# A transformer block on one core: convolution sums moved to PSUM, gate projections issued earlier, expert selection in fewer and wider vector operations

## The chip, the cores and the metric

The kernel runs on one core of a Trainium2 chip. The metric is the device time of one execution in microseconds (us), the median of the runs that are shown. Five engines run their own instruction streams and wait for each other: PE (matrix products), DVE and POOL (elementwise work), ACT (elementwise functions and scaling), and SP (starts most transfers).

## What is computed

One encoder layer over 512 tokens of width 1024, all in float32, followed by a retrieval layer over 16384 one-neuron experts:

```python
h = rmsnorm(x)
z = h @ w_in            # [conv input 2*1024 | q 16x64 | k 4x64 | v 4x64 | 2 gates 2*1024]
u = z[:1024] * sigmoid(z[1024:2048])
u = depthwise_conv(u, width=31) + bias;  u = silu(layernorm(u));  A = u @ w_pw
B = windowed_attention(q, k, v, |t-s| <= 128, ALiBi bias, sink) @ w_o
x = x + (sigmoid(gate_A) * A + sigmoid(gate_B) * B) @ w_out
# retrieval: 8 heads, two keys of 128 each
q = rmsnorm(x) @ w_query;  sc = q . sub_keys            # (t, head, 2, 128)
vals, idx = top_k(sc, 16)                                # per key
top_s, pos = top_k(vals0[:, None] + vals1[None, :], 16)  # of 16x16 pairs
expert = idx0[pos // 16] * 128 + idx1[pos % 16];  gate = softmax(top_s)
x = x + sum_k gate_k * gelu(u[expert_k] . h) * v[expert_k]
out = rmsnorm(x)
```

## The kernel before

Every float32 product is made of three passes (`mm3`, lines 61 to 66): both operands are split into a rounded part `hi` (ACT, line 58) and the rest `lo` (line 59, on POOL, on DVE in some places), and PE sums hi·hi, hi·lo and lo·hi in PSUM. One projection of 128 columns (`proj`, line 167) is 24 matmuls of 512 columns.

**Front.** `glu(i)` (line 191) projects the two halves of a 128-channel block of the convolution input, and DVE multiplies them into `ub` (line 200). `conv(pair, ubs)` (line 203) then makes 31 taps for two channel blocks in turn, one DVE instruction per tap and block:

```python
DVE.scalar_tensor_tensor(acc, ub[:, j:j + S], tapt[:, i, j:j + 1], acc,
                         op0=OP.mult, op1=OP.add)          # acc = cv[:, i, :], in SBUF
```

Eight blocks give 240 of these (line 211) and 8 first taps (line 208). Between the pairs stand the projections of k, v (lines 215 to 233) and q (`qproj`, line 235). `attend(g, b)` (line 253) is attention for four heads and 128 queries: scores to PSUM (`s`), a DVE custom instruction that adds the bias and takes the maximum (line 267), exponentials on ACT (275), a scaling by the reciprocal sum on DVE (282), transposes on PE (287) and the product with v (`o`). The bias tables are made on POOL (line 250). Behind attention come the layer norm of the convolution, 16 gate projections (`gate`, line 240, evicted by ACT into `sg`), the projections with `w_o` and `w_pw` (lines 350 and 388) and the output projection (`out_half`).

**Retrieval, preparation.** `qproj2` and `score` fill `sct` per head. For tokens 128 to 511, DVE finds the top 16 (`topk`), and `select(t, q)` (line 469) turns positions into expert indices by a one-hot table `oh` of 16 positions by 64 entries, once per key: compare (487), multiply by the index (490), sum (496). `build(t)` (line 570) makes one-hot rows for 8 tokens (594, 595), scales them (596, 597), and PE multiplies them into gate tables, which go to DRAM.

**Retrieval, main part.** All 128 blocks of experts are multiplied for these tokens (`u_block`, `v_block`): 30 u blocks run ahead, beside the preparation. For tokens 0 to 127 rows are gathered instead (`step`).

Order of work: a scheduler orders each engine's stream by priority in program order, and an engine then runs its stream in order. `tc.high_priority()` moves a few DVE operations ahead. [...]

## Time and profile before

| | us |
|---|---|
| three runs | 1873.26, 1873.43, 1878.59 |
| median | 1873.43 |
| profiled execution, its own time | 1870.83 |
| its span (first to last instruction) | 1869.1 |

| stretch of the span | what PE does |
|---|---|
| to 27.75 | load, first norm, first glu |
| 27.75 to 275 | projections; DVE convolves |
| 275 to 406.6 | attention; DVE's last convolution taps are at 286; gate projections in between |
| 406.6 to 520.9 | rest of the gates, w_o, w_pw |
| 520.9 to 595 | output projection, second norm |
| 595 to 912 | query projections, top-k, selection, one-hot tables |
| 912 to the end | expert blocks and gathered rows |

A row of the profile gives an instruction group's line, engine, operation, the tile written and the tiles read, its shape and count, its busy time, the mean time of one, and the idle time just ahead of it with what ended it.

### The profile page before, as it was taken

The numbers are of one execution on the slowest core, as the hardware profiler recorded it, in microseconds if no ns is written. First come the engines' busy times: TensorE is split into PE (matmuls) and PEld (weight loads), VectorE is DVE, ScalarE is ACT, GpSimd is POOL, SyncE is SP. The second block draws the span as 40 slices with busy tenths as digits, with TensorE's granted clock in tenths as the row PEclk, the third lists the DMA queues.
The fourth block names the chain that finished last, engine by engine and source line by source line (L and its number), as shares of the span: only waits on it lengthen the run. The fifth ranks groups of instructions, "written<-read, shape, count | busy, mean of one in ns | idle before, by whom it ended". The sixth has DMA issues, their size and how long they took to land.

```text
span 1869.1 us, 25289 instructions
## 1 busy us (share of the span) xinstructions
PE 1751.3 (94%) x8873; PEld 1495.0 (80%) x8873; DVE 1536.5 (82%) x2649; ACT 753.2 (40%) x1329; POOL 1049.0 (56%) x757
## 2 busy tenths in 40 slices
PE   7878879999999986887899999999999999999998
PEld 5656656778887876776889899999999999999886
DVE  5999978854534999999798899998988977797874
ACT  4222325865224414554443333333333333333243
POOL 4544373231015525465535788788887888787611
PEclk9999889999999999999999999999999999999999
DMA  4122111034234202468866989898998888887972
GB/s 152 58 77 75 61 46 35 12 92 167 68 102 150 88 26 93 137 191 253 275 221 239 340 320 337 297 330 317 325 336 306 330 311 316 313 314 292 351 270 97
DMA packets 148943, 379.43 MB, mean 203 GB/s; under 512 B 11520, under 2 KB 63760, under 8 KB 148816
## 3 DMA queue, kind: packets, MB, share of 16 engines
q1 hardware_dynamic: 110832, 241.20, 37.2%
q0 software_dynamic: 37120, 134.52, 20.3%
q10 hardware_dynamic: 864, 2.10, 0.3%
q8 instruction: 69, 1.13, 0.2%
q14 instruction: 58, 0.48, 0.1%
HBM read 346.84 MB, written 30.93 MB: 202 GB/s over the span
## 4 chain that ended last, share of the span: by engine, by line
PE 40%; DVE 14%; DMA 5%; issue 2%; POOL 2%; ACT 1%; SPq 0%; POOLq 0%; DVEq 0%; ACTq 0%
PE acc L65 7%; PE acc L66 7%; PE acc L64 7%; PE hps L66 6%; PE hps L64 6%; PE hps L65 6%; DVE oi L594 1%; DVE ohi L596 1%; DVE olo L597 1%; DVE oj L595 1%; DVE vlo L59 1%; DMA row<-in_v_dram,eidx 1%; DMA vraw<-in_v_dram 1%; DVE ij L496 1%; POOL ulo L59 1%
## 5 line engine op out<-in xcount | busy, mean ns | idle before, releaser
L59 POOL TENSOR_TENSOR ulo<-uraw,uhi 128x512 fp32r<-128x512 f32 x256 | 423.8, 1671 | 279.7 <-ACT uhi L58 262.9
L64 PE MATMUL hps<-big,uhi 128*128 128x384 f32 x1024 | 350.9, 343 | 7.8 <-ACT hb L429 7.7
L66 PE MATMUL hps<-big,ulo 128*128 128x384 f32 x1024 | 350.2, 342 | 2.6 <-POOL ulo L59 2.6
L65 PE MATMUL hps<-big,uhi 128*128 128x384 f32 x1024 | 349.4, 341 | 0.0
L59 POOL TENSOR_TENSOR wlo<-wraw,whi 128x512 fp32r<-128x512 f32 x120 | 194.8, 1631 | 231.5 <-ACT whi L58 205.6
L65 PE MATMUL acc<-vlo,ph 128*128 128x512 f32 x768 | 300.2, 391 | 2.0 <-DVE vlo L59 2.0
L64 PE MATMUL acc<-vhi,ph 128*128 128x512 f32 x768 | 298.9, 390 | 1.2 <-ACT vhi L58 1.2
L66 PE MATMUL acc<-vhi,pl 128*128 128x512 f32 x768 | 299.6, 390 | 0.0
L64 PE MATMUL mm<-big,whi 128*128 128x512 f32 x544 | 224.2, 412 | 28.0 <-DVE ub L200 12.4
L58 ACT ACTIVATE uhi<-uraw 128x512 fp32r<-128x512 f32 x256 | 155.5, 629 | 206.7 <-DMA uraw<-in_ut_dram 83.9
L641 DVE SCALAR_TENSOR_TENSOR yacc<-row,dots,yacc 128x1024 f32<-128x1024 f32 x127 | 189.2, 1490 | 58.0 <-DMA row<-in_v_dram,eidx 57.7
L66 PE MATMUL mm<-big,wlo 128*128 128x512 f32 x544 | 220.2, 405 | 14.5 <-POOL wlo L59 14.4
L630 DVE SCALAR_TENSOR_TENSOR row<-row,h2tok 128x1024 f32<-128x1024 f32 x128 | 193.9, 1521 | 34.6 <-DMA row<-in_u_dram,eidx 33.9
L58 ACT ACTIVATE vhi<-vraw 128x1024 fp32r<-128x1024 f32 x128 | 135.0, 1055 | 212.3 <-DMA vraw<-in_v_dram 200.2
L65 PE MATMUL mm<-big,whi 128*128 128x512 f32 x544 | 220.0, 404 | 0.0
L211 DVE SCALAR_TENSOR_TENSOR cv<-ub,tapt,cv 128x512 f32<-128x512 f32 x240 | 212.1, 930 | 1.8
L58 ACT ACTIVATE whi<-wraw 128x512 fp32r<-128x512 f32 x152 | 94.7, 631 | 287.4 <-PE mm L65 169.7
L64 PEld LDWEIGHTS hps<-big,uhi 128*128 128x128 f32 x1024 | 195.1, 191 | 15.4 <-ACT hb L429 8.7
L623 POOL DMA_INDIRECT row<-in_v_dram,eidx x128 | 176.3, 1377 | 49.3 <-DVE yacc L641 20.3
L623 POOL DMA_INDIRECT row<-in_u_dram,eidx x128 | 182.9, 1429 | 33.1 <-issue 17.5
L65 PEld LDWEIGHTS hps<-big,uhi 128*128 128x128 f32 x1024 | 195.5, 191 | 4.1
L66 PEld LDWEIGHTS hps<-big,ulo 128*128 128x128 f32 x1024 | 194.8, 190 | 3.6 <-POOL ulo L59 3.6
(217 smaller groups left out, 3027.0 us busy)
## 6 DMA issues: line engine op xcount, KB each, us to landing
uraw<-in_ut_dram SPq DMA_DIRECT2D x128, 512.0 KB, 7.1
vraw<-in_v_dram SPq DMA_DIRECT2D x128, 512.0 KB, 5.5
gates_dram<-st SPq DMA_DIRECT2D x12, 2048.0 KB, 9.9
gt<-gates_dram SPq DMA_DIRECT2D x32, 768.0 KB, 7.0
wraw<-in_w_in_dram SPq DMA_DIRECT2D x44, 512.0 KB, 3.3
wraw<-in_w_query_dram SPq DMA_DIRECT2D x16, 512.0 KB, 3.4
oraw<-in_w_out_dram SPq DMA_DIRECT2D x16, 256.0 KB, 3.1
wraw<-in_w_o_dram SPq DMA_DIRECT2D x8, 512.0 KB, 3.8
```

Source lines behind the costliest of these rows:

```text
L58: ACT.activation(hi, src, AF.Copy)
L59: lo_engine.tensor_tensor(lo, src, f(hi), op=OP.subtract)
L64: PE.matmul(ps, wh, mh, start=first and i == 0, stop=False)
L65: PE.matmul(ps, wh, ml, start=False, stop=False)
L66: PE.matmul(ps, wl, mh, start=False, stop=last and i == n - 1)
L211: DVE.scalar_tensor_tensor(acc, ub[:, j:j + S], tapt[:, i, j:j + 1], acc, op0=OP.mult, op1=OP.add)
L496: DVE.tensor_reduce(ij[t][:, s, hs, :].rearrange("p h k -> p (h k)"), oh.rearrange("p a h k -> p (h k) a"), AX.X, OP.add)
L594: DVE.tensor_tensor(prs(oi), iota8, row(0), op=OP.is_equal)
L595: DVE.tensor_tensor(prs(oj), iota8, row(1), op=OP.is_equal)
L623: POOL.indirect_dma_start(out=row, out_offset=None, in_=table, in_offset=bass.IndirectOffsetOnAxis(ap=eidx[:, c:c + 1], axis=0))
L630: DVE.scalar_tensor_tensor(row, row, 1.0, h2tok, op0=OP.mult, op1=OP.mult, accum_out=dots[:, c:c + 1])
L641: DVE.scalar_tensor_tensor(yacc, row, dots[:, c:c + 1], yacc, op0=OP.mult, op1=OP.add)
```

## The change

1. The convolution's running sum lives in PSUM (pool `psc`, two banks); only the last tap writes `cv` in SBUF. `glu` takes its two PSUM tiles from attention's score pool. The pool `pso` for attention's output is opened only after all convolutions, in `psc`'s place.
2. `glu` of the next pair stands ahead of `conv` of this one; the 16 gate projections are spread: 11 between the convolutions (`fill`), 5 within attention.
3. The bias tables go from POOL to ACT, and half of the scalings by the reciprocal sum from DVE to ACT.
4. `select` handles both keys in one compare, one multiply and one sum, with the 16 positions innermost (neighbouring) in `oh`; the index to compare with is written twice in a row (`fd`).
5. `build` joins the two compares into one of 2048 elements.

```diff
         def proj(src, rhs, ws=None, lo_engine=POOL, ps=None):
...
-            pso = ac.enter_context(tc.tile_pool(name="pso", bufs=1, space=PSUM))
-
             glup = ExitStack()
+            psc = glup.enter_context(tc.tile_pool(name="psc", bufs=2, space=PSUM))
...
-                pa = proj(w_in[i], hT, first if i == 0 else None)
-                pg = proj(w_in[8 + i], hT)
+                pa = proj(w_in[i], hT, first if i == 0 else None, ps=psa.tile([P, S], F32, name="s"))
+                pg = proj(w_in[8 + i], hT, ps=psa.tile([P, S], F32, name="s"))
...
             def conv(pair, ubs):
+                accs = [psc.tile([P, S], F32, name="ca") for _ in pair]
                 for j in range(TAPS):
-                    for i, ub in zip(pair, ubs):
-                        acc = cv[:, i, :]
+                    for i, ub, acc in zip(pair, ubs, accs):
...
-                            DVE.scalar_tensor_tensor(acc, ub[:, j:j + S], tapt[:, i, j:j + 1], acc,
-                                                     op0=OP.mult, op1=OP.add)
-
-            conv((0, 1), [glu(0), glu(1)])
+                            DVE.scalar_tensor_tensor(cv[:, i, :] if j == TAPS - 1 else acc, ub[:, j:j + S],
+                                                     tapt[:, i, j:j + 1], acc, op0=OP.mult, op1=OP.add)
+
+            ub01 = [glu(0), glu(1)]
+            conv((0, 1), ub01)
+            ub23 = [glu(2), glu(3)]
...
-                    POOL.tensor_scalar(bt[:, i, :], dist, -8.0 * slope, None, op0=OP.mult)
+                    ACT.activation(bt[:, i, :], dist, AF.Copy, scale=-8.0 * slope)
...
                 for i in range(4):
-                    DVE.tensor_scalar(L[:, i, :n], L[:, i, :n], rd[:, i:i + 1], None, op0=OP.mult)
+                    if i % 2:
+                        ACT.activation(L[:, i, :n], L[:, i, :n], AF.Copy, scale=rd[:, i:i + 1])
+                    else:
+                        DVE.tensor_scalar(L[:, i, :n], L[:, i, :n], rd[:, i:i + 1], None, op0=OP.mult)
...
-            conv((2, 3), [glu(2), glu(3)])
+            gates = [gate_of for k in range(KD) for gate_of in (KD + k, k)]
+
+            def fill(n):
+                for _ in range(n):
+                    gate(gates.pop(0))
+
             for i in range(4):
                 qproj(i)
-            conv((4, 5), [glu(4), glu(5)])
+            conv((2, 3), ub23)
+            ub45 = [glu(4), glu(5)]
             for i in range(4, 8):
                 qproj(i)
-            conv((6, 7), [glu(6), glu(7)])
+            fill(3)
+            conv((4, 5), ub45)
+            ub67 = [glu(6), glu(7)]
+            fill(6)
+            conv((6, 7), ub67)
+            fill(2)
+            glup.close()
+            pso = ac.enter_context(tc.tile_pool(name="pso", bufs=1, space=PSUM))
             for g in range(4):
                 make_bias(g)
                 for b in range(NT):
                     attend(g, b)
-            glup.close()
+                    if b == 1 or (g, b) == (0, 3):
+                        fill(1)
...
-            for k in range(KD):
-                gate(KD + k)
             sigmoid(1)
-            for k in range(KD):
-                gate(k)
...
-            DVE.tensor_tensor(fa, fa, bits[:, 0:2, :], op=OP.add)
...
-            for s in range(2):
-                oh = sel.tile([P, TOPK, HH, TOPK], F16, name="oh", bufs=2)
-                DVE.tensor_tensor(oh.rearrange("p a h k -> p a (h k)"), iota16,
-                                  fa[:, s, None, :].to_broadcast([P, TOPK, nk]), op=OP.is_equal)
...
-                DVE.tensor_reduce(ij[t][:, s, hs, :].rearrange("p h k -> p (h k)"),
-                                  oh.rearrange("p a h k -> p (h k) a"), AX.X, OP.add)
+            fd = sel.tile([P, 2, nk, 2], F16, name="fd", bufs=2)
+            DVE.tensor_tensor(fd, fa[:, :, :, None].to_broadcast([P, 2, nk, 2]),
+                              bits[:, 0:2, :, None].to_broadcast([P, 2, nk, 2]), op=OP.add)
...
+            oh = sel.tile([P, 2, HH, TOPK, TOPK], F16, name="oh", bufs=2)
+            DVE.tensor_tensor(oh.rearrange("p s h k (a b) -> p (s h k) a b", b=2),
+                              iota16.rearrange("p (a b) -> p a b", b=2)[:, None].to_broadcast([P, 2 * nk, TOPK // 2, 2]),
+                              fd.rearrange("p s n b -> p (s n) b")[:, :, None, :].to_broadcast([P, 2 * nk, TOPK // 2, 2]),
+                              op=OP.is_equal)
+            oh3 = oh.rearrange("p s h k a -> p (s h) k a")
+            DVE.tensor_tensor(oh3, oh3, ixf.rearrange("p s h a -> p (s h) a")[:, :, None, :]
+                              .to_broadcast([P, 2 * HH, TOPK, TOPK]), op=OP.mult)
+            DVE.tensor_reduce(ij[t][:, 0:2, hs, :].rearrange("p s h k -> p s (h k)"),
+                              oh.rearrange("p s h k a -> p s (h k) a"), AX.X, OP.add)
...
-                    DVE.tensor_tensor(prs(oi), iota8, row(0), op=OP.is_equal)
-                    DVE.tensor_tensor(prs(oj), iota8, row(1), op=OP.is_equal)
-                    DVE.tensor_tensor(prs(oh_), prs(oj), row(2), op=OP.mult)
-                    DVE.tensor_tensor(prs(ol), prs(oj), row(3), op=OP.mult)
+                    DVE.tensor_tensor(prs(oij), iota8, rows(0), op=OP.is_equal)
+                    for s in range(2):
+                        DVE.tensor_tensor(prs(ohl)[:, s * TB8:(s + 1) * TB8], prs(oij)[:, TB8:],
+                                          rows(2)[:, s * TB8:(s + 1) * TB8], op=OP.mult)
```

What moves, in the order in which the engines issue. DVE of the kernel before, where the scores of the first attention block meet the convolution of blocks 4 and 5 (`L,m<-s` is the bias and maximum, `ub<-mm` the product of a glu):

```order
L211 SCALAR_TENSOR_TENSOR cv<-ub,tapt,cv 128x512 x13
L267 ISA L,m<-s,bias,sinkt 128x256
L267 ISA m 128x1
L200 TENSOR_TENSOR ub<-mm,sgm 128x512
L211 SCALAR_TENSOR_TENSOR cv<-ub,tapt,cv 128x512
L208 TENSOR_SCALAR cv<-ub,tapt,dwb 128x512
L211 SCALAR_TENSOR_TENSOR cv<-ub,tapt,cv 128x512 x6
```

These attention operations stood between the taps; in the change none does. DVE of the change, the last pair of blocks and the first attention operation:

```order
L209 SCALAR_TENSOR_TENSOR ca<-ub,tapt,ca 128x512 x13
L198 TENSOR_TENSOR ub<-s,sgm 128x512
L209 SCALAR_TENSOR_TENSOR ca<-ub,tapt,ca 128x512
L206 TENSOR_SCALAR ca<-ub,tapt,dwb 128x512
L209 SCALAR_TENSOR_TENSOR ca<-ub,tapt,ca 128x512 x30
L209 SCALAR_TENSOR_TENSOR cv<-ub,tapt,ca 128x512
L209 SCALAR_TENSOR_TENSOR ca<-ub,tapt,ca 128x512 x14
L209 SCALAR_TENSOR_TENSOR cv<-ub,tapt,ca 128x512
L267 ISA L,m<-s,bias,sinkt 128x256
```

Before, 120 of the 248 taps stood ahead of the first attention operation and 128 among attention; now all 248 stand ahead of it. PE's stream follows: before, 432 projection matmuls precede the first score, now 936; within attention it holds 144 (511 before), and after attention 360 of the front's (497 before).

ACT of the change, from the last q projection (`qh`) to the sigmoids of the last two glus (`sgm`); `sg` are gate evictions, `whi` weight splits:

```order
L57 ACTIVATE qh<-mm 128x512
L57 ACTIVATE whi<-wraw 128x512 x2
L242 ACTIVATE sg_83<-mm 128x512
L57 ACTIVATE whi<-wraw 128x512 x2
L242 ACTIVATE sg_82<-mm 128x512
L57 ACTIVATE whi<-wraw 128x512 x2
L242 ACTIVATE sg_83<-mm 128x512
L57 ACTIVATE whi<-wraw 128x512 x4
L193 ACTIVATE sgm<-s 128x512
L57 ACTIVATE whi<-wraw 128x512 x4
L193 ACTIVATE sgm<-s 128x512
```

Three gate evictions stand ahead of the last two glus, and eight more follow them before the first exponential; before the change no gate came ahead of the last glu.

## Rows read from the trace of the kernel before

**Rows 1.** The page: busy time of PE and DVE, and three rows of 40 slices.

```profile
PE 1751.3 (94%) x8873; PEld 1495.0 (80%) x8873; DVE 1536.5 (82%) x2649; ACT 753.2 (40%) x1329; POOL 1049.0 (56%) x757
...
PE   7878879999999986887899999999999999999998
...
DVE  5999978854534999999798899998988977797874
...
PEclk9999889999999999999999999999999999999999
```

**Rows 2.** Windows: start:end, length, then busy us (instructions) of each engine; PEclk.

```profile
core 0: us, PE busy (x) PEld busy (x) DVE busy (x) ACT busy (x) POOL busy (x), PEclk, DMA share, GB/s
27.75:275.00 247.25, 202.94 (x807) 156.65 (x806) 230.51 (x291) 61.17 (x105) 124.35 (x74) 0.91 0.20 67
275.00:406.60 131.60, 130.23 (x602) 90.76 (x602) 113.00 (x309) 94.40 (x227) 34.56 (x25) 1.00 0.09 28
406.60:520.90 114.30, 114.30 (x500) 93.51 (x500) 46.49 (x70) 49.74 (x76) 18.05 (x14) 1.00 0.37 121
520.90:595.00 74.10, 72.26 (x343) 59.38 (x342) 28.36 (x44) 30.79 (x60) 24.35 (x19) 1.00 0.42 142
...
640.00:912.00 272.00, 224.59 (x1634) 193.69 (x1633) 266.72 (x680) 120.35 (x220) 141.34 (x94) 0.94 0.47 142
...
950.00:1850.00 900.00, 897.98 (x4467) 808.26 (x4467) 770.22 (x878) 338.92 (x537) 649.82 (x452) 1.00 0.84 304
```

**Rows 3.** PE's waits from 25 to 275 us: total us, times, longest.

```profile
PE mm L66 <- POOL wlo L59: 13.9, 1, 13.9
PE mm L64 <- DVE ub L200: 12.4, 4, 6.7
PE mm L64 <- DVE ql L59: 8.0, 5, 3.1
```

**Rows 4.** DVE's longest wait in the same stretch.

```profile
DVE ql L59 <- ACT qh L58: 13.4, 1, 13.4
```

**Rows 5.** Line 211, the taps: ns minimum/median/maximum.

```profile
L211 DVE SCALAR_TENSOR_TENSOR cv<-ub,tapt,cv x240: 733/747/1789, 30.5 to 286.3; 128x512 f32<-128x512 f32 x120
```

**Rows 6.** DVE's timeline: start us, us in all, instructions; three runs of taps.

```profile
30.53 14.68 DVE L211 SCALAR_TENSOR_TENSOR cv<-ub,tapt,cv 128x512 f32<-128x512 f32 x14
...
56.27 4.71 DVE L211 SCALAR_TENSOR_TENSOR cv<-ub,tapt,cv 128x512 f32<-128x512 f32 x7
...
231.34 23.94 DVE L211 SCALAR_TENSOR_TENSOR cv<-ub,tapt,cv 128x512 f32<-128x512 f32 x36
```

**Rows 7.** POOL's timeline: weight splits, a lone one and four around 235 us.

```profile
53.16 1.38 POOL L59 TENSOR_TENSOR wlo<-wraw,whi 128x512 fp32r<-128x512 f32 x1 [0.95 <-ACT whi L58]
...
234.52 26.50 POOL L59 TENSOR_TENSOR wlo<-wraw,whi 128x512 fp32r<-128x512 f32 x4 [7.74 <-ACT whi L58]
```

**Rows 8.** Groups by line and shape: DVE operations that read PSUM.

```profile
L200 DVE TENSOR_TENSOR ub<-mm,sgm 128x512 f32<-128x512 f32 x8 | 5.5, 684 | 8.3 <-ACT sgm L195 8.3
L104 DVE SCALAR_TENSOR_TENSOR big<-mm,g,big 128x512 fp32r<-128x512 f32 x8 | 5.4, 747 | 2.7 <-ACT big L103 2.7
```

**Rows 9.** Groups: the reciprocal scaling, and a comparable operation on ACT.

```profile
L282 DVE TENSOR_SCALAR L<-L,rd 128x384 f32<-128x384 f32 x32 | 16.1, 553 | 0.1
L275 ACT ACTIVATE L<-L,nm 128x384 f32<-128x384 f32 x32 | 19.3, 610 | 1.3 <-DVE nm L270 1.1
```

**Rows 10.** Selection's operations: ns minimum/median/maximum.

```profile
L487 DVE TENSOR_TENSOR oh<-iota,fa x16: 671/690/1787, 647.0 to 990.2; 128x1024 f16<-128x1024 f16 x16
L490 DVE TENSOR_TENSOR oh<-oh,ixf x16: 1211/1220/2315, 648.2 to 993.0; 128x1024 f16<-128x1024 f16 x16
L496 DVE TENSOR_REDUCE ij<-oh x16: 1847/2022/2074, 650.5 to 996.1; 128x64 f32<-128x1024 f16 x16
L503 DVE TENSOR_REDUCE gs<-ij x8: 204/210/223, 654.4 to 987.3; 128x4 f32<-128x64 f32 x8
```

**Rows 11.** The one-hot compare of the table build, in the same form.

```profile
L594 DVE TENSOR_TENSOR oi<-iotar,tt x48: 677/683/1792, 748.0 to 907.1; 128x1024 f16<-128x1024 f16 x48
```

More of the change, by code (lines that the diff above doesn't have):

```diff
@@ L37 @@
 UQ, UB = 2, 4
-SELE = "DD"
 LAST = 3
@@ L165, in encoder_block, with proj @@
         hT = [(hT_hi[:, k, :], hT_lo[:, k, :]) for k in range(KD)]
-        def proj(src, rhs, ws=None, lo_engine=POOL):
+        def proj(src, rhs, ws=None, lo_engine=POOL, ps=None):
             ws = ws or weights(src, lo_engine)
-            ps = psm.tile([P, S], F32, name="mm")
+            ps = psm.tile([P, S], F32, name="mm") if ps is None else ps
             mm3(ps, ws, rhs)
@@ L481, in select @@
             DVE.tensor_tensor(fa, fa, bits[:, 4, None, :].to_broadcast([P, 2, nk]), op=OP.mult)
-            DVE.tensor_tensor(fa, fa, bits[:, 0:2, :], op=OP.add)
-            ixf = sel.tile([P, HH, 2, TOPK], F16, name="ixf", bufs=2)
-            DVE.tensor_copy(ixf, idxs[t][:, hs])
-            for s in range(2):
-                oh = sel.tile([P, TOPK, HH, TOPK], F16, name="oh", bufs=2)
-                DVE.tensor_tensor(oh.rearrange("p a h k -> p a (h k)"), iota16,
-                                  fa[:, s, None, :].to_broadcast([P, TOPK, nk]), op=OP.is_equal)
-                if SELE[q] == "D":
-                    DVE.tensor_tensor(oh, oh, ixf[:, :, s, :].rearrange("p h a -> p a h")[:, :, :, None]
-                                      .to_broadcast([P, TOPK, HH, TOPK]), op=OP.mult)
-                else:
-                    for h in range(HH):
-                        POOL.tensor_tensor(oh[:, :, h, :], oh[:, :, h, :],
-                                           ixf[:, h, s, :, None].to_broadcast([P, TOPK, TOPK]), op=OP.mult)
-                DVE.tensor_reduce(ij[t][:, s, hs, :].rearrange("p h k -> p (h k)"),
-                                  oh.rearrange("p a h k -> p (h k) a"), AX.X, OP.add)
@@ L573, in build, with twice @@
                 PE.transpose(tp[:, s, :], ij[t][:, s].rearrange("p h k -> p (h k)"), ident)
-            def twice(ap):
-                return ap[..., None].to_broadcast(list(ap.shape) + [2])
-            tt = gw.tile([P, 4, P, 2], F16, name="tt", bufs=2)
-            ACT.activation(tt[:, 0:2], twice(tp[:, 0:2, :]), AF.Copy)
-            ACT.activation(tt[:, 2], twice(tp[:, 2, :]), AF.Copy, scale=GSC)
-            DVE.scalar_tensor_tensor(tt[:, 3], twice(tp[:, 2, :]), GSC, tt[:, 2], op0=OP.mult, op1=OP.subtract)
+            def twice(s):
+                a = tp[:, s, :].rearrange("p (g t) -> p g t", t=TB8)
+                return a[..., None].to_broadcast([P, P // TB8, TB8, 2])
+            tt = gw.tile([P, P // TB8, 4, TB8, 2], F16, name="tt", bufs=2)
+            for s in range(3):
+                ACT.activation(tt[:, :, s], twice(s), AF.Copy, scale=1.0 if s < 2 else GSC)
+            DVE.scalar_tensor_tensor(tt[:, :, 3], twice(2), GSC, tt[:, :, 2], op0=OP.mult, op1=OP.subtract)
             for c in range(P // GT):
@@ L585, in build, with rows @@
                     n = c * GT + q8 * TB8
-                    oi, oj, oh_, ol = (gw.tile([P, TB8, NKEY], F16, name=nm, bufs=2) for nm in ("oi", "oj", "ohi", "olo"))
-                    def row(s):
-                        return tt[:, s, n:n + TB8, None, :].to_broadcast([P, TB8, NKEY // 2, 2])
+                    oij, ohl = (gw.tile([P, 2, TB8, NKEY], F16, name=nm, bufs=2) for nm in ("oij", "ohl"))
+                    def rows(s):
+                        a = tt[:, n // TB8, s:s + 2].rearrange("p s t b -> p (s t) b")
+                        return a[:, :, None, :].to_broadcast([P, 2 * TB8, NKEY // 2, 2])
                     def prs(a):
-                        return a.rearrange("p t (a b) -> p t a b", b=2)
-                    DVE.tensor_tensor(prs(oi), iota8, row(0), op=OP.is_equal)
-                    DVE.tensor_tensor(prs(oj), iota8, row(1), op=OP.is_equal)
-                    DVE.tensor_tensor(prs(oh_), prs(oj), row(2), op=OP.mult)
-                    DVE.tensor_tensor(prs(ol), prs(oj), row(3), op=OP.mult)
+                        return a.rearrange("p s t (a b) -> p (s t) a b", b=2)
+                    DVE.tensor_tensor(prs(oij), iota8, rows(0), op=OP.is_equal)
+                    for s in range(2):
+                        DVE.tensor_tensor(prs(ohl)[:, s * TB8:(s + 1) * TB8], prs(oij)[:, TB8:],
+                                          rows(2)[:, s * TB8:(s + 1) * TB8], op=OP.mult)
                     for q4 in range(TB8 // 4):
```

13 lines of the change are left out of this document (7 added, 6 removed).

## The prediction

> **What bounds the kernel now.** I read the page first: PE is busy 94% of the span and DVE 82%, and the slices show that they take turns [rows 1]. From 25 to about 275 us and again from 640 to 910 us DVE stands at 9 while PE falls to 6 to 8; elsewhere PE stands at 9. Then I cut the span into stretches [rows 2]. [...] From 275 to 595 us PE is busy practically without a gap. From 640 to 912 us DVE works 267 of 272 us and PE 225. From 950 us on PE is busy 898 of 900 us; so whatever is saved ahead of that shifts the rest forward by as much, and nothing in the change touches the rest.
>
> **Why DVE is slow in the first stretch.** Of the 240 taps the fastest take 733 ns, the slowest 1789 [rows 5]. Seven of them take 4.71 us, 0.67 each from start to start, in a stretch where POOL is idle (its weight split ends at 54.5 us, the next starts after 62); fourteen beside POOL's weight splits take 14.68 us, 1.05 each [rows 6, 7]. At 231 us DVE runs 36 taps without a gap at 0.665 each, and in that time POOL needs 26.5 us for four splits, against 1.4 us for one [rows 6, 7]. PE waits 13.9 us for the last of them, and DVE itself then 13.4 us for attention behind it [rows 3, 4]. So an operation with two SBUF inputs on DVE and POOL's splits hold each other up, in both directions. DVE's operations with one input in PSUM show no such spread: the glu product takes 684 ns [rows 8].
>
> **The change part by part.** The sum is made against the profiled execution, 1870.8 us; the median of the runs shown is 2.6 us above it.
>
> *Taps in PSUM.* 240 taps keep their number; 232 now read and write PSUM and the last of each block writes SBUF. No row has DVE writing PSUM. Nearest is line 104, the same operation with a PSUM input and an SBUF output, 747 ns [rows 8], 14 ns above the fastest tap [rows 5]. From below, a tap can cost 0.60 from start to start (the shortest step in these rows: 684 ns of the glu product less the 0.08 by which successive operations overlap: 747 against 0.67); from above 1.05, as beside POOL today. I take 0.70, near line 104. [...]
>
> *Projections up to attention.* In the change's order, 936 projection matmuls stand before the first score, 48 of them done at 27.75 us as now. The other 888, with the 8 transposes of v, at the pace of a full PE (500 in 114.3 us, 0.2286 each [rows 2]) take 204.8 us. A glu needs its tiles back from DVE before the next one starts; before, PE lost 12.4 us to that in four waits [rows 3], and I charge 10 us. So PE would reach the first score at 27.75 + 204.8 + 10 = 242.6 us. DVE has until then: it starts at 30 us and has 240 taps of 0.70 plus about 20 us of first taps, glu products and lo parts (some 30 operations of about 0.65), which ends at 218 us without waits. The last glu is ready at about 199 us (242.6 less eight gates of 24 x 0.2286); 47 taps follow it, to 232 us. So PE is the bound here, as long as a tap costs under 0.80 (by DVE's whole work) to 0.93 us (by the last 47 taps). Eleven gates hide DVE's taps instead of standing alone later.
>
> *Attention.* In the change it holds 144 projection matmuls, 192 scores, 160 transposes, 120 products with v and 20 records of the layer norm's matmuls (the trace shows each as two): 636. The present stretch of that kind made 602 in 131.6 us, 0.2186 each [rows 2]; so 139 us. DVE gets lighter: no taps among its operations, and 32 of the 64 scalings, 553 ns for the wider ones, leave [rows 9]. ACT gets 32 scalings and 16 bias tables, at about 0.6 us each going by its exponential [rows 9], some 29 us on top of 94 of 132 us [rows 2], less about 11 us of layer norm work that now comes after attention: 112 of 139. I add 7 us for the waits that this closeness brings, as no row prices them. The bias tables leave POOL, which was no bound there (35 of 132 us).
>
> *After attention.* 360 matmuls of w_o and w_pw at 0.2286 take 82.3 us, and 12 records of the layer norm 2.7. The rest of the layer norm (about 20 us on DVE and ACT) runs beside the 168 matmuls of w_o (38 us), as does the first sigmoid. The output projection starts at 242.6 + 139 + 7 + 85 = 473.6 instead of 520.9 us: **47 us earlier**. From there to 595 us nothing changes.
>
> *Selection.* Six of the eight calls lie in the DVE-bound stretch up to 912 us; the other two lie beside a full PE and cost nothing either way. Compare and multiply work on the same 1024 elements; the first makes two a step (neighbours in 16 bits), the second one: 671 and 1211 ns [rows 10]. The difference, 540 ns for 512 steps, is 1.05 ns a step, and 131 ns are fixed. In the change both have neighbouring positions, so both take 1024 steps for 2048 elements: 1211 ns. The sum over positions reads them 128 bytes apart today, 1847 ns at best: 1.68 ns a step [rows 10]. The small contiguous sum of line 503 gives (210 - 131) / 64 = 1.2 ns a step. For 2048 that is between 2.59 and 3.56 us; I take 2.6, since the new layout is contiguous like line 503's. Doubling the indices (`fd`, 256 elements instead of 128, one a step) adds about 0.14. A call goes from 2 x (0.67 + 1.21 + 1.85) = 7.46 to 1.21 + 1.21 + 2.6 + 0.14 = 5.16: 2.3 us saved, 14 us for six. At the upper price of the sum it is 1.3 a call, 8 us. Each operation may also lose 1.1 us to POOL (the maxima of the compare [rows 10]), and there are three instead of six of them: up to 7 us more. [...]
>
> *Table build.* 48 times two compares of 683 ns [rows 11] become one of 1211: 0.155 us by durations, about 0.07 from start to start since neighbours overlap by 0.08. Between 3 and 7 us; I take 3. The two remaining multiplications stay, and so do POOL's splits, which hold up whatever runs beside them. PE has 47 us free in the DVE-bound stretch [rows 2], so 17 us come through.
>
> Sum: 1870.8 - 47 - 14 - 3 = 1807 us in the profiled execution, 1809 for the median.
>
> **The rivals.**
> 1. *Attention becomes the bound.* Today its chains (scores, maximum, exponential, scaling, transposes, split) are filled by 511 projection matmuls and partly hidden under the taps; the change leaves 144 and none of the taps. For it: ACT at 112 of 139 us. Against: DVE has less to do, and PE's stretch held without idle time. If an instruction costs 0.26 instead of 0.2186, 26 us are lost: 1835 us for the median.
> 2. *The taps still collide with POOL.* Only if it is not the second SBUF input that collides. Then the mean of today, 930 ns or so between 0.67 and 1.05, stays: taps end at 50 + 223 = 273 us, the output projection starts 231 us later, at 504: 17 + 17 us gained, 1839 us for the median. Against it: the steady 684 ns of [rows 8].
> 3. *Slower: a running sum in PSUM is dear.* Each tap reads what another wrote two instructions ago, now through PSUM, and attention can no longer start before the last tap, as it does today. The output projection starts at 281 + 240 p; with the 17 us of the second part, the change loses when p exceeds 1.07 us. At 1.5 us it starts at 641: 1870.8 + 120 - 17 = 1974 us, 1976 for the median. For it: no row has DVE writing PSUM. Against it: line 104 reads PSUM for 14 ns.
> 4. *PE keeps its full pace throughout.* Without the 17 us of waits I charged and with attention's matmuls at 0.2 each (12 us), the upper ends of selection (7) and build (4) on top: 40 us below the forecast, 1769 us.
>
> **How the numbers follow.** The forecast gets 0.60; rival 1 0.15, rival 2 0.09, rival 4 0.09, rival 3 0.05, and 0.02 that a wait cancels everything. The forecast's own unknowns are -10 (the lower end of selection and waits) to +15 us (rival 4's terms in part). The range of 8 in 10 reaches from rival 4's end to rivals 1 and 2 with a few us of spread, 1770 to 1842 us, and leaves out rival 3. Faster by over 0.3% (5.6 us, about what a measurement of this kernel tells from no change): 0.60 + 0.15 + 0.09 + 0.09, about 0.92; slower 0.05; the same 0.03.
>
> **What would show it.** Right: taps with minimum and maximum within 50 ns of each other, at about 0.75 us; POOL's splits at 1.3 us with no 26 us group; the first score at about 243 us on PE and the output projection near 474; selection's sum as one operation of 2.3 to 2.7 us, its multiplication at 1.2; the stretch of tables about 17 us shorter; from there the same 920 us or so to the end. Wrong: taps over 1 us (rivals 2 and 3, told apart by their spread); PE idle in attention behind ACT or DVE (rival 1); a sum of 3.5 us. The prediction is off in its mechanism if the front ends before 520 us for another reason than PE's closed gaps, or if the time saved ahead of 950 us is not found at the end.

## The result, and the profile after

The changed kernel takes 1815.0 us (median of four runs, 1813.0 to 1818.5) against 1876.0 us for the kernel before on the same chip (four runs: the three shown above and 1880.7): a ratio of 0.967, 95% interval 0.965 to 0.970. The forecast was 1809 us, with a range of 1770 to 1842. On another chip (e11 below) the changed kernel took 1813.0 us, and the kernel before stood between 1872.2 and 1873.2 us in all three groups of experiments; so their medians are compared with 1813.0.

The page of the changed kernel, for [rows 1]: busy time, and three rows of 40 slices.

```profile
PE 1734.4 (96%) x8873; PEld 1484.2 (82%) x8873; DVE 1432.8 (79%) x2545; ACT 770.8 (43%) x1374; POOL 961.4 (53%) x741
...
PE   6999999989999978888999999999999999999998
...
DVE  4999856674536999999989987887787777878874
...
PEclk8999999999999989999999999999999999999999
```

In the first third PE now stands at 9 nearly throughout, and DVE only in the second to the fourth slice. The seven and the four eights of PE under the nines of DVE (634 to 860 us) are still there. The windows of the same kernel, cut where its own stages end, answer to [rows 2]:

```profile
0.00:27.75 27.75, 13.54 (x52) 10.76 (x53) 9.50 (x20) 15.86 (x29) 11.28 (x26) 0.82 0.54 180
...
27.75:243.50 215.75, 210.56 (x926) 172.12 (x925) 183.60 (x271) 65.34 (x113) 99.12 (x85) 1.00 0.28 93
243.50:382.90 139.40, 136.99 (x637) 95.64 (x637) 92.72 (x289) 113.37 (x274) 9.05 (x7) 1.00 0.07 23
382.90:477.40 94.50, 90.81 (x374) 70.71 (x373) 53.54 (x78) 41.19 (x65) 10.51 (x8) 0.98 0.36 117
...
477.40:551.50 74.10, 72.93 (x347) 60.18 (x347) 28.39 (x45) 31.50 (x61) 24.30 (x19) 1.00 0.42 142
...
597.00:855.00 258.00, 217.83 (x1619) 186.65 (x1618) 257.88 (x675) 119.32 (x220) 120.56 (x98) 0.96 0.49 151
...
892.00:1792.00 900.00, 898.39 (x4470) 808.54 (x4469) 728.77 (x822) 341.13 (x536) 640.30 (x449) 1.00 0.83 303
```

Up to the first score PE works 210.6 of 215.8 us at the full clock (before: 202.9 of 247.3 at 0.91), in attention 137.0 of 139.4. The 74.1 us behind the start of the output projection and the 900 us to the end hold the same work as before (347 and 4470 records of PE against 343 and 4467 [rows 2]; a record is one matmul in the trace). PE's one wait in the second window is this:

```profile
PE s L63 <- ACT sgm L193: 5.2, 5, 1.0
```

The 13.9, 12.4 and 8.0 us of [rows 3] are gone; what is left is a wait for the sigmoid of a glu on ACT. The groups of line or shape, ns minimum/median/maximum, first and last start, of taps (209), scores and output projection (63), selection (501 to 508) and table build (607, 609):

```profile
L209 DVE SCALAR_TENSOR_TENSOR ca<-ub,tapt,ca x232: 735/752/756, 37.0 to 233.7; 128x512 f32<-128x512 f32 x116
L209 DVE SCALAR_TENSOR_TENSOR cv<-ub,tapt,ca x8: 739/745/748, 73.4 to 234.5; 128x512 f32<-128x512 f32 x8
...
L63 PE MATMUL s<-kh,qh x64: 275/381/442, 243.5 to 364.3; 64*128 64x256 f32 x32, 64*128 64x384 f32 x32
...
L63 PE MATMUL mm<-ohi,qh x64: 389/392/486, 477.4 to 521.7; 128*128 128x512 f32 x64
...
L501 DVE TENSOR_TENSOR oh<-iota,fd x8: 1201/1214/2331, 602.8 to 914.1; 128x2048 f16<-128x2048 f16 x8
...
L506 DVE TENSOR_TENSOR oh<-oh,ixf x8: 1201/1212/2187, 604.1 to 918.4; 128x2048 f16<-128x2048 f16 x8
...
L508 DVE TENSOR_REDUCE ij<-oh x8: 2260/2270/2272, 605.5 to 920.6; 128x128 f32<-128x2048 f16 x8
...
L607 DVE TENSOR_TENSOR oij<-iotar,tt x48: 1209/1214/2320, 687.6 to 847.6; 128x2048 f16<-128x2048 f16 x48
...
L609 DVE TENSOR_TENSOR ohl<-oij,tt x96: 665/680/1769, 691.8 to 850.4; 128x1024 f16<-128x1024 f16 x96
```

The taps' spread of 733 to 1789 ns [rows 5] has become 735 to 756. The output projection starts at 477.4 instead of 520.9 us, 43.4 us earlier; the profiled execution is 57.9 us shorter (1870.8 to 1813.0), so 14.5 us come from behind it.

### The profile page after: what moved, and what is told of

Same layout as the page of the kernel before. It is cut to its first block, busy times and chain, and to the rows that moved or that the text cites. A ratio compares the mean times of both kernels' runs of the same rounds, so it can differ in the third digit from the quotient of the medians.

```text
span 1811.2 us, 25192 instructions
## 1 busy us (share of the span) xinstructions
PE 1734.4 (96%) x8873; PEld 1484.2 (82%) x8873; DVE 1432.8 (79%) x2545; ACT 770.8 (43%) x1374; POOL 961.4 (53%) x741
## 4 chain that ended last, share of the span: by engine, by line
PE 68%; DVE 15%; issue 2%; DMA 2%; ACT 1%; POOL 1%; SPq 0%; POOLq 0%; DVEq 0%; ACTq 0%
PE acc L64 8%; PE acc L63 8%; PE acc L65 8%; PE hps L65 7%; PE hps L64 7%; PE hps L63 7%; PE mm L63 5%; PE mm L65 5%; PE mm L64 4%; DVE ohl L609 4%; DVE oij L607 3%; DMA row<-in_v_dram,eidx 1%; PE s L63 1%; PE pt L290 1%; PE s L64 1%
## 5 line engine op out<-in xcount | busy, mean ns | idle before, releaser
L58 POOL TENSOR_TENSOR ulo<-uraw,uhi 128x512 fp32r<-128x512 f32 x256 | 406.1, 1595 | 290.6 <-ACT uhi L57 271.0
L58 POOL TENSOR_TENSOR wlo<-wraw,whi 128x512 fp32r<-128x512 f32 x120 | 157.8, 1318 | 203.5 <-ACT whi L57 202.0
L57 ACT ACTIVATE uhi<-uraw 128x512 fp32r<-128x512 f32 x256 | 160.1, 631 | 233.6 <-PE hps L64 140.9
L654 DVE SCALAR_TENSOR_TENSOR yacc<-row,dots,yacc 128x1024 f32<-128x1024 f32 x127 | 177.2, 1396 | 69.7 <-DMA row<-in_v_dram,eidx 69.4
L58 DVE TENSOR_TENSOR vlo<-vraw,vhi 128x1024 fp32r<-128x1024 f32 x128 | 188.6, 1474 | 18.9 <-ACT vhi L57 18.9
L636 POOL DMA_INDIRECT row<-in_v_dram,eidx x128 | 165.1, 1290 | 48.7 <-DVE yacc L654 21.5
L57 ACT ACTIVATE ph<-hb 128x384 fp32r<-128x384 f32 x128 | 66.8, 523 | 287.4 <-PE acc L64 274.6
L65 PEld LDWEIGHTS acc<-vhi,pl 128*128 128x128 f32 x768 | 144.2, 188 | 30.9 <-DVE pl L58 0.3
L64 PEld LDWEIGHTS acc<-vlo,ph 128*128 128x128 f32 x768 | 144.2, 188 | 30.0 <-DVE vlo L58 3.7
L63 PEld LDWEIGHTS acc<-vhi,ph 128*128 128x128 f32 x768 | 144.1, 188 | 28.4 <-ACT vhi L57 1.0
```

Of the source, the lines that this page charges most:

```text
L57: ACT.activation(hi, src, AF.Copy)
L58: lo_engine.tensor_tensor(lo, src, f(hi), op=OP.subtract)
L63: PE.matmul(ps, wh, mh, start=first and i == 0, stop=False)
L64: PE.matmul(ps, wh, ml, start=False, stop=False)
L65: PE.matmul(ps, wl, mh, start=False, stop=last and i == n - 1)
L636: POOL.indirect_dma_start(out=row, out_offset=None, in_=table, in_offset=bass.IndirectOffsetOnAxis(ap=eidx[:, c:c + 1], axis=0))
```

## The experiments

The theory on trial: the sum in PSUM frees DVE and POOL from each other; PE then bounds the front, as long as the gates are there to fill it; selection and build save about what their durations say. A starting time of the output projection (start, below) is the start of line 63's group with `ohi`, in the profiled execution; of the same kernel it was 477.4 and 480.4 us, so 3 us of it mean nothing. For the tables there is a second measure: from start to the first product of `v_block` (first start of `acc<-vhi,ph`) it takes 412.5 us in the kernel before, 397.8 and 397.2 in the two traces of the changed kernel, and 397.7 to 399.8 in the seven runs below that leave the tables alone (e1, e2, e5, e6, e8, e9, e10). From there to the last product every run takes 921 to 930 us.

**e1, the taps' sum back in SBUF.**

```diff
-  scalar_tensor_tensor(cv[:, i, :] if j == TAPS - 1 else acc, ub[:, j:j + S], tapt[:, i, j:j + 1], acc, ...)
+  scalar_tensor_tensor(acc if j == TAPS - 2 else cv[:, i, :], ub[:, j:j + S], tapt[:, i, j:j + 1],
+                       acc if j == TAPS - 1 else cv[:, i, :], ...)
```

> The changed kernel with the taps' running sum back in SBUF; only the last two taps go through the PSUM tile, so that its bank is held as long as before, and everything else (order, gates, attention, selection, tables) stays. Theory of the prediction: a second SBUF input on DVE and POOL's splits hold each other up, so taps spread from 733 to about 1790 ns with a mean near 0.9 us start to start, POOL's weight splits rise again over 1.5 us, DVE becomes the bound before attention (240 x 0.9 + 20 us from 37 us), the first score falls from 243 to about 270 us, and the time goes from 1815 to about 1842 us (1830 to 1850). Rival, the gain of the front comes from the new order of the projections alone: first score within 4 us of 243, time 1812 to 1819 us.

Measured: 1869.0 us, 56 more than the changed kernel (ratio to before 0.997, 0.996 to 0.999). Its taps, where the front ends, and the window of attention's first 27 us:

```profile
L209 DVE SCALAR_TENSOR_TENSOR cv<-ub,tapt,cv x224: 734/744/1881, 38.3 to 291.5; 128x512 f32<-128x512 f32 x112
...
L209 DVE SCALAR_TENSOR_TENSOR ca<-ub,tapt,cv x8: 747/749/1836, 78.7 to 292.3; 128x512 f32<-128x512 f32 x8
L209 DVE SCALAR_TENSOR_TENSOR cv<-ub,tapt,ca x8: 734/738/748, 80.0 to 293.1; 128x512 f32<-128x512 f32 x8
...
L63 PE MATMUL mm<-ohi,qh x64: 389/392/486, 533.7 to 578.0; 128*128 128x512 f32 x64
```

```profile
283.00:310.00 27.00, 17.29 (x57) 12.86 (x57) 17.09 (x39) 8.25 (x23) 1.81 (x1) 0.62 0.07 20
```

The spread is back with the second SBUF input. The eight taps that read PSUM do not have it (748 at most, in the same stretch, though eight are few); the eight that read SBUF twice and write PSUM do (1836). The theory holds in kind and was too cheap: the first score came at 283 us, not 270, and start is 533.7, 13 us later than before the change. Up to there the new order without the PSUM sum is worse than the old one.

**e2, the gates written behind attention.**

```diff
-            fill(3)            # and fill(6), fill(2), fill(1) in attention
+            for k in range(KD):          # behind the layer norm
+                gate(KD + k)
             sigmoid(1)
+            for k in range(KD):
+                gate(k)
```

> The changed kernel with the sixteen gate projections back behind attention, where the kernel before had them; taps stay in PSUM. Theory of the prediction: the PSUM sum only shortens DVE's work, and the gates have to be there for PE to fill it; without them DVE (240 x 0.67 + 20 us, from 37 us) bounds the front, first score at about 220 to 225 us, attention with 517 records bound by ACT's 110 us of work at about 125 us, then 88 us of gates with the layer norm hidden under them and 85 us up to the output projection: it starts at about 520 instead of 477 us, time 1855 us (1845 to 1875), so nearly all of the 43 us lost. Rival, the PSUM sum is the gain by itself and the gates' place is worth little: 1815 to 1830 us.

Measured: 1811.0 us (0.966, 0.963 to 0.969), no difference to the changed kernel; start 474.5. The theory's number failed, and the time is below the rival's 1815 to 1830 us as well. The evictions of the gates, and two windows about the end of DVE's taps, say why:

```profile
L242 ACT ACTIVATE sg<-mm x16: 578/580/600, 191.0 to 387.2; 128x512 f32<-128x512 f32 x16
```

```profile
200.00:225.00 25.00, 25.00 (x112) 20.71 (x111) 25.00 (x39) 8.12 (x14) 12.19 (x10) 1.00 0.29 94
225.00:250.00 25.00, 25.00 (x104) 16.30 (x103) 15.08 (x51) 16.75 (x35) 3.98 (x4) 1.00 0.12 43
```

PE made its first two scores at 184.7 us and could not go on with attention before DVE's first attention operation at 225.5. Into that time the scheduler itself put eight gates, evicted from 191 to 229 us, and PE does not stand. So this run changed the text and hardly PE's order; e9 changes the order.

**e9, the same, with the order tied.** Each gate's first matmul is tied behind the attention matmul written before it.

```diff
+   tc.keep_in_program_order(PE.matmul(ps, ws[0][0], hT[0][0], start=True, stop=False))
```

> As e2_gates_last, but each gate's first matmul is tied behind the attention matmul written last before it, so that PE's order has no gate before the first score (in e2 some were still put there by the scheduler). Theory, PE needs the gates while DVE does its taps: about 600 projection matmuls of 0.2274 us end at about 165 us, taps (0.67 each, DVE full) only at about 220 us, PE stands up to 55 us, the output projection starts at 505 to 523 instead of 477 us, time 1840 to 1860 us. Rival, attention's scores fill the gap and the order is worth nothing: 1809 to 1818 us.

Measured: 1855.1 us (0.992, 0.989 to 0.995), 42 more than the changed kernel and within the theory's range. PE's longest wait, two windows, and start:

```profile
PE s L63 <- DVE m L272: 40.0, 1, 40.0
```

```profile
200.00:225.00 25.00, 0.00 (x0) 0.00 (x0) 25.00 (x39) 0.00 (x0) 0.00 (x0) 0.50 0.00 0
225.00:250.00 25.00, 23.82 (x55) 14.17 (x56) 14.17 (x49) 9.14 (x30) 0.00 (x0) 0.50 0.00 1
```

```profile
L63 PE MATMUL mm<-ohi,qh x64: 389/392/477, 521.2 to 565.5; 128*128 128x512 f32 x64
```

PE stands for 40 us while DVE makes taps without a gap (25 of 25 us), and then runs 25 us at a granted clock of 0.50, in which e2 had 104 records and this kernel 55. Start is 521.2: that of the kernel before (520.9). With e1 this settles the front: taps in PSUM without gates to fill PE give nothing (521), gates without taps in PSUM give nothing (534), both give 477. That `glu` of the next pair stands ahead of `conv` of this one is the same in both; what this is worth by itself no run shows.

**e3, the old selection.** Each key by itself, positions outermost, as in the lines that the change removes.

```diff
-            oh = sel.tile([P, 2, HH, TOPK, TOPK], F16, name="oh", bufs=2)
+            for s in range(2):
+                oh = sel.tile([P, TOPK, HH, TOPK], F16, name="oh", bufs=2)
```

> The changed kernel with the selection of the kernel before (each key by itself, positions outermost). Theory of the prediction, with the sum as measured (2.27 us): the six calls in the DVE-bound stretch cost what they cost before, 14 to 20 us more, time 1829 to 1835 us, and the stretch of the tables longer by the same. Rival, the stretch is bound by PE or POOL already and the selection is covered: 1812 to 1819 us.

Measured: 1829.7 us (0.977, 0.974 to 0.979), 16.7 more. Start is 477.4 as in the changed kernel, so the difference arises behind it, where the theory has it: the stretch to the first product of `v_block` takes 416.9 us instead of 397.2 to 399.8. The old sum's group in this run, and the new one's in the changed kernel, from 560 to 912 us (busy us, mean ns | idle before):

```profile
L505 DVE TENSOR_REDUCE ij<-oh 128x64 f32<-128x1024 f16 x14 | 27.4, 1995 | 0.0
```

```profile
L508 DVE TENSOR_REDUCE ij<-oh 128x128 f32<-128x2048 f16 x7 | 15.9, 2268 | 0.0
```

For seven calls the sums alone take 11.5 us less.

**e4, the compare of the build in two.**

```diff
-  DVE.tensor_tensor(prs(oij), iota8, rows(0), op=OP.is_equal)
+  for s in range(2):
+      DVE.tensor_tensor(prs(oij)[:, s * TB8:(s + 1) * TB8], iota8[:, :TB8],
+                        rows(0)[:, s * TB8:(s + 1) * TB8], op=OP.is_equal)
```

> The changed kernel with the joined compare of the table build split again into two compares of 1024 elements; all else stays. Theory of the prediction: 0.07 to 0.16 us for each of 48, 3 to 7 us, time 1818 to 1822 us. Rival A, each instruction meets POOL's splits once, so one instruction less per step saves its collision too: by the means (2 x 0.81 of before against 1.46) 8 us, time about 1823 us. Rival B, the collisions only move to the multiplications behind (their mean rose from 864 to 912 ns): no change, 1812 to 1817 us.

Measured: 1818.4 us, 5.4 more by the medians (1813.0 for e11); the ratios to the kernel before (0.970, both) do not separate them. Start is 480.8, as in e11. DVE's 48 steps take 159.8 us of busy time, 6.5 more than in the changed kernel (153.3); a step is what `build` makes for eight tokens. In the second trace of the changed kernel (e11) the same steps take 151.0 us. The compares and multiplications here (mean 819 and 920 ns by their groups), and the products of `v_block` here and in the changed kernel:

```profile
L608 DVE TENSOR_TENSOR oij<-iotar,tt x96: 677/679/1779, 690.7 to 856.9; 128x1024 f16<-128x1024 f16 x96
...
L611 DVE TENSOR_TENSOR ohl<-oij,tt x96: 666/679/1770, 694.3 to 859.2; 128x1024 f16<-128x1024 f16 x96
```

```profile
L63 PE MATMUL acc<-vhi,ph x768: 388/389/499, 884.9 to 1809.6; 128*128 128x512 f32 x192
```

```profile
L63 PE MATMUL acc<-vhi,ph x768: 387/389/506, 875.2 to 1802.6; 128*128 128x512 f32 x192
```

From start to the first of these products it is 404.1 us, 4 to 7 more than in the kernels with the joined compare (397.2 to 399.8). So 3 to 7 us is borne out by the medians and by this stretch, and rival B's nothing is not; no closer figure is. Rival A's 8 us lies just above.

**e7, the multiplications joined as well.**

```diff
-  for s in range(2):
-      DVE.tensor_tensor(prs(ohl)[:, s * TB8:(s + 1) * TB8], prs(oij)[:, TB8:], rows(2)[...], op=OP.mult)
+  oj2 = oij[:, 1, None].to_broadcast([P, 2, TB8, NKEY]).rearrange("p s t (a b) -> p s t a b", b=2)
+  hl2 = tt[:, n // TB8, 2:4, :, None, :].to_broadcast([P, 2, TB8, NKEY // 2, 2])
+  DVE.tensor_tensor(ohl.rearrange("p s t (a b) -> p s t a b", b=2), oj2, hl2, op=OP.mult)
```

> The changed kernel with the two remaining multiplications of the table build joined too (column compare read twice by a step of zero, row factors in pairs): one instruction of 2048 elements in place of two of 1024. Theory of the prediction, fixed cost alone: 2 x 665 against 1209 ns, start to start 0.04 to 0.12 us for each of 48, 2 to 6 us faster, 1809 to 1813 us. Rival A, a collision with POOL is paid once an instruction: 2 x 0.91 against 1.46 us, 17 us of DVE and up to 15 us of time, 1800 us. Rival B, the third dimension breaks the pairs and it makes one element a step: 2.27 against 1.33 us, 45 us slower, 1860 us.

Measured: 1818.2 us (0.971, 0.969 to 0.973): no gain, 5.2 more than e11 by the medians. A miss for the theory and for both rivals. The joined operations, and PE's wait for them from 560 to 912 us, here and in the changed kernel:

```profile
L607 DVE TENSOR_TENSOR oij<-iotar,tt x48: 1190/1282/2292, 689.9 to 850.4; 128x2048 f16<-128x2048 f16 x48
...
L610 DVE TENSOR_TENSOR ohl<-oij,tt x48: 1195/1201/2310, 693.9 to 851.8; 128x2048 f16<-128x2048 f16 x48
...
PE gp L615 <- DVE ohl L610: 33.5, 32, 2.9
```

```profile
PE gp L615 <- DVE ohl L609: 24.5, 26, 2.3
...
PE gp L616 <- DVE ohl L609: 3.6, 4, 1.0
```

Pairs are kept (1195 ns for 2048 elements, where 1024 without neighbouring positions took 1211 [rows 10]), and DVE's 48 steps get shorter by 3 to 5 us (148.3 us busy instead of 153.3, or 151.0 in e11). But PE's first product now waits for the whole joined operation, 33.5 us in all instead of 28.1 (27.7 in e11), and the stretch from start to the first product of `v_block` stays at 398.0 us. So the tables gain nothing, and the 5.2 us of the medians do not arise in them: they lie in the main part, which the edit does not touch (929.9 us against 927.4 and, in e11, 925.0). The compare's mean rose from 1457 (1381 in e11) to 1657 ns; e12 shows where such time comes from.

**e12, without POOL's splits beside the build.** For the first 30 blocks of u the low parts are left out.

```diff
+            if i < LEAD:
+                ACT.activation(hi, raw[:, ks, :], AF.Copy)
+                lo = hi
+            else:
+                split(hi, lo, raw[:, ks, :], POOL)
```

> The changed kernel without POOL's splits for the first 30 blocks of u (their low parts are left out, the high part is multiplied again in their place, so the number of matmuls stays). Theory, what the joined operations do not save is the time that DVE and POOL's splits take from each other: the 48 steps lose about 0.7 us each to 50 such splits, 34 us in all. Without them the joined compare has a mean of 1.25 us at most (1.46 before) and the multiplications 0.70 (0.91), DVE's stretch of the tables falls from 258 to about 225 us, where PE (218 us) bounds it, and the time to 1780 to 1795 us. Rival, the long instances come from transfers or from ACT: the means stay, and the time at 1808 to 1818 us.

Measured: 1775.4 us (0.949, 0.947 to 0.952), 38 less than the changed kernel, a little more gained than the theory had. The stretch from start to the first product of `v_block` falls to 358.1 us, so all of it arises there. Compare and multiplication, and the window of the tables:

```profile
L611 DVE TENSOR_TENSOR oij<-iotar,tt x48: 1197/1214/1311, 685.2 to 812.0; 128x2048 f16<-128x2048 f16 x48
L613 DVE TENSOR_TENSOR ohl<-oij,tt x96: 661/678/686, 687.5 to 813.9; 128x1024 f16<-128x1024 f16 x96
```

```profile
597.00:825.00 228.00, 217.17 (x1675) 192.35 (x1674) 225.36 (x705) 125.99 (x230) 44.34 (x52) 0.98 0.59 182
```

The long instances are gone (longest compare 1311 ns instead of 2320, longest multiplication 686 instead of 1769), and the last multiplication starts at 813.9 instead of 850.4 us. It is POOL's splits that make them long. Of the changed kernel's operations with one input in SBUF the selection's sum stays within 2260 to 2272 ns (line 508 above), but not every one does: the shift of line 490 takes 179 to 1293 ns, with a median of 184. What each step of eight tokens loses, the sum of mean less minimum over its operations, hardly depends on how many operations a step has: 0.64 us with four operations (before), 0.79 with four (e4), 0.74 with three (after), 0.71 with two (e7), and 0.05 without the splits.

**e5, biases and scalings back.**

```diff
-  ACT.activation(bt[:, i, :], dist, AF.Copy, scale=-8.0 * slope)
+  POOL.tensor_scalar(bt[:, i, :], dist, -8.0 * slope, None, op0=OP.mult)
-  if i % 2:
+  if False:
```

> The changed kernel with the bias tables back on POOL and all 64 reciprocal scalings back on DVE. Theory of the prediction: POOL was no bound in attention, DVE had room, PE bounds the stretch; attention stays at 139 us within 3 us and the time at 1811 to 1818 us. Rival, moving work to ACT was needed: without it DVE holds attention up, 5 to 15 us slower. Rival on the other side, ACT at 113 of 139 us holds PE up now: 3 to 8 us faster, 1807 to 1812 us.

Measured: 1822.5 us (0.974, 0.971 to 0.976), 9.5 more; start 484.2. The window of attention in this run:

```profile
243.40:388.90 145.50, 142.50 (x638) 97.12 (x638) 108.12 (x324) 95.83 (x232) 23.41 (x19) 0.99 0.07 22
```

Attention takes 145.5 instead of 139.4 us for the same PE instructions, with DVE at 108 instead of 93 us and ACT at 96 instead of 113. PE is not seen to wait for DVE for more than 2.5 us in it, so how the 6 us divide is open. In time the first rival holds, and part of the gain is the work moved to ACT, for which the prediction had no term; that it is DVE that holds attention up is not shown, and the bias tables and the scalings were not put back one by one. The runs of this kernel spread from 1818 to 1827 us; the profiled one, 1818.2, is 5.2 above the changed kernel's profiled one (1813.0), about what attention lost.

**e6, the first glu in the old pool.**

```diff
+  pa, pg = (None if i == 0 else psa.tile([P, S], F32, name="s") for _ in range(2))
-  pa = proj(w_in[i], hT, first if i == 0 else None, ps=psa.tile([P, S], F32, name="s"))
+  pa = proj(w_in[i], hT, first if i == 0 else None, ps=pa)
```

> The changed kernel with the first glu's two sums in the pool mm again, as before the change, instead of the score pool, whose banks are those of the first transposes and come free only when the last of them is read. [...] Rival, DVE or the layer norm sets the front's end: the start moves but the output projection does not, 1812 to 1818 us.

Measured: 1806.2 us (0.964, 0.962 to 0.967 to before), 6.8 less than the changed kernel and below the 1808 to 1810 us that were expected of an earlier first matmul; start 471.8. PE's timeline at the start, here and in the changed kernel (start, us in all, instructions):

```profile
15.75 0.50 PE L63 MATMUL mm<-big,whi 128*128 128x512 f32 x1 [1.18 <-ACT big L102]
```

```profile
20.91 0.79 PE L63 MATMUL s<-big,whi 128*128 128x512 f32 x1 [2.64 <-DVE big L103]
```

The change gave the first glu its banks from the score pool, which is opened where the pool of the first transposes was closed; so its first matmul waited for the last of those to be read (DVE, line 103) instead of running between them.

**e8, a product ahead of the reciprocal.** In the stretch between attention and the output projection, the first projection with `w_o` is written ahead of the layer norm's reciprocal, which is tied behind its product.

```diff
+            for j in range(1):
+                w_o_mul(j)
...
-            DVE.reciprocal(rs, rs)
+            tc.keep_in_program_order(DVE.reciprocal(rs, rs))
```

> The changed kernel with the first product of the attention projection with its gate put ahead of the layer norm's reciprocal on DVE, which waits 5.6 us for ACT's square root and holds that product, and so PE's next tile, up. [...] Rival, the layer norm's chain ends the stretch anyway: the reciprocal comes later, w_pw waits for it, no gain, 1813 to 1820 us.

Measured: 1813.2 us (0.968, 0.966 to 0.970), no gain, where 1809 to 1811 us were expected; start 477.0. PE's wait from 383 to 470 us here, two of its windows, and the wait in the changed kernel:

```profile
PE mm L63 <- DVE sg L354: 3.6, 1, 3.6
```

```profile
396.00:402.00 6.00, 5.07 (x22) 3.77 (x20) 6.00 (x9) 5.39 (x8) 2.55 (x2) 1.00 0.57 168
402.00:410.00 8.00, 5.34 (x17) 4.38 (x18) 7.69 (x14) 6.86 (x12) 0.00 (x0) 0.79 0.30 92
```

```profile
PE mm L63 <- DVE sg L365: 2.5, 2, 1.9
PE mm L65 <- DVE wlo L58: 1.0, 1, 1.0
```

The wait moved a few us back with all its length: DVE works 6.00 of 6.00 us there on the layer norm, and the next product stands behind that instead.

**e10, e2 and e6 together.**

> e2 and e6 together: first glu in the pool mm, and the gates written behind attention (the scheduler spreads them, so that matmuls are left to run beside the layer norm). Theory: the start gives 5 to 6 us as in e6, and the layer norm no longer stops PE (e2 lost nothing there, e6 4.6 us and some 3 at the lower clock), so the output projection starts at about 468 us, time 1800 to 1806 us, below e6. Rival, the two gains are the same idle time: as e6, 1805 to 1808 us.

Measured: 1805.5 us (0.965, 0.963 to 0.967); start 472.1. The time lies in the theory's range and in the rival's; start decides for the rival, 472.1 against 471.8 in e6 and 468 in the theory: the gain of the first glu is there, and nothing on top. PE's last blocks of attention show where it went:

```profile
330.00:364.50 34.50, 30.11 (x130) 20.68 (x129) 20.57 (x59) 27.76 (x68) 3.84 (x3) 0.90 0.05 16
```

Up to attention's end at 364.5 us PE is without work for 4.4 us, at a granted clock of 0.90; behind it PE does not stand, where e6 waits 4.6 us for DVE.

**e11, the changed kernel again.**

> The changed kernel itself beside the two above on one chip, for a comparison without another chip's shift: 1811 to 1816 us, a ratio of 0.965 to 0.970 to the kernel before.

Measured: 1813.0 us (0.970, 0.968 to 0.972). Start 480.4, last matmul of the main part at 1802.6 us, as in its first profile. e6 and e10, whose intervals lie below this one, beat both kernels; of e10's two edits only that of e6 counts.

## Why the prediction was right, point by point

*Front: 47 us forecast, 43.4 measured.* The mechanism was right, as e1 and e9 show together: taps last 752 ns (0.75 among the signs), 0.67 us from start to start (0.70 in the sum), PE bounds, first score at 243.5 (242.6). That this met so closely is luck: two errors cancel.
- "48 of them done at 27.75 us as now" failed. The bank of the first glu came late; 20 records were done (52 with the 32 transposes, the first window above), which is 28 x 0.2286 = 6.4 us; e6 gets 6.8 back. I had followed the pools for the taps and not for the first glu.
- The 10 us charged for handing glu tiles back were 5.2, and PE waited for ACT in them, not for DVE.
- Attention: 139.4 us where I had 139 + 7. ACT's estimate of 112 us came out at 113.4. The charge for waits was not needed, but rival 1 was not far: with biases and scalings as before the change (e5) attention takes 6 us more.
- After attention: 94.5 us, 85 forecast. "The rest of the layer norm runs beside the matmuls of w_o" is the step that failed: PE stands 3.7 us, runs about 2 us behind after it (17 records from 396 to 402 us at a granted clock of 0.72), and the layer norm's own records take 0.47 us each (8 in 3.72), not 0.2286, 3 us for 12. The window and the records in the changed kernel:

```profile
396.00:402.00 6.00, 5.50 (x17) 4.38 (x18) 6.00 (x9) 4.99 (x7) 2.39 (x2) 0.72 0.56 147
```

```profile
383.13 3.72 PE L345 MATMUL ln<-sq,ones 128*128 128x512 f32 x8
```

"Eleven gates hide DVE's taps" was right of PE's order (e9), but the new places in the text were not needed for it: with the gates written last the scheduler puts eight into the same gap by itself (e2).

Taps that read and write PSUM have a median of 752 ns, those with all operands in SBUF 747 [rows 5]: 5 ns more.

*Selection: 14 us forecast (8 to 21).* e3 gives 16.7. The term mis-sized is the sum: 2.6 us forecast, 2.27 measured; (2268 - 131) / 2048 is 1.04 ns a step. My row, a sum of 64 elements, was too short to carry a price per step. Compare and multiplication, forecast at 1211 ns, measured 1214 and 1212. Of the "up to 7 us more" from losing less to POOL, which no sum gives (three operations fewer, 1.1 us each, six calls would be 20), about 3 are seen: over the six calls of the stretch, mean less minimum of compares and multiplications fell from 9.0 to 1.8 us in all, but a small operation behind them, which took 206 to 222 ns before, now loses 4.0 us (its median is 212 ns again without POOL's splits, e12):

```profile
L517 DVE TENSOR_TENSOR ij<-ij,gs x8: 207/604/1321, 607.7 to 922.8; 128x64 f32<-128x64 f32 x8
```

*Build: 3 us forecast (3 to 7).* e4 gives 5.4 by the medians and 4 to 7 by the stretch. That fewer operations would lose less to POOL, the remark made for the selection (each "may also lose 1.1 us to POOL"), does not hold for the build: the loss a step stays (e7, e12).

*Together behind the output projection:* 17 forecast; 14.5 in one profiled execution, 17.4 in the other (1339.6 us from its start to the last matmul before, 1325.2 and 1322.2 after). Taken one at a time (e3, e4) the parts come to 16.7 and 5.4, 22 us: they do not add up, and why is open.

*Rivals.* Rival 2 (taps still collide) did not happen, and e1 shows what it would have been: 1869, not 1839. Of the 30 us, 10 lie ahead of the first score (283 instead of 273), 9 in attention (155.2 us instead of 139 + 7; PE stands 9.7 us at its start, and the granted clock up to 310 us is 0.62), and 10 behind it (95.5 instead of 85), where the forecast failed too. Rival 3 (dear sums in PSUM) is excluded by the taps' 735 to 756 ns. Rival 4 (full pace) was right that attention needs no charge for waits, but not of its pace: 637 records in 139.4 us are 0.219 each, as in the forecast, and not 0.2.

That DVE with two SBUF inputs and POOL hold each other up was read from the rows, and e1 and e12 agree: longest tap 1881 against 756 ns, longest compare 2320 against 1311.

## What to carry to other kernels

An engine freed from a collision gains only what the next engine has work for (start 521.2 us in e9, 477.4 with the gates in place): take the two edits apart by PE's order, not by the text, because a scheduler may already have moved the work (e2: eight gates). When POOL's splits run beside DVE, joining DVE's operations didn't reduce what DVE loses to them in the table build (0.71 to 0.79 us a step); the sum in PSUM instead of SBUF (e1: longest tap 756 ns instead of 1881) and fewer splits (e12: 0.05 us a step) did. When a tile changes its pool, look at who held those banks last, for its first use as well (e6: first matmul at 15.75 us instead of 20.91).

## What was not expected of the hardware

- In the table build the time that DVE loses to POOL's splits stays at 0.64 to 0.79 us a step whether two, three or four DVE operations share it, and falls to 0.05 without the splits.
- A multiplication of 2048 two-byte elements whose one operand is read twice by a step of zero, with five dimensions in the pattern, takes 1195 ns at best (e7); two of 1024 elements without the second reading take 665 ns each in the changed kernel.
- An instruction that reads and writes PSUM (tap, 752 ns) and one with all operands in SBUF (747 ns) cost nearly the same.
